# Big runs of 16256 columns in place of 16384 in a streaming binary cross entropy

## The chip, the cores and the metric

One core of a Trainium2 chip. The time is that of the device in microseconds, median of several executions. Verdicts are by ratio at 2%. A ratio is the mean time of one kernel's runs over that of the other's runs of the same rounds, so it is not quite the ratio of the medians that are quoted.

Words used below: SBUF is the core's memory on the chip. In the views DVE is VectorE, ACT is ScalarE, POOL is GpSimd and SP is SyncE. All transfers are issued by POOL or SP, each on a queue of its own, and the core's 16 transfer (DMA) engines work for both queues. The page is the summary of one profiled execution; it cuts the span into 40 equal slices and gives busy shares in tenths. A table by stretches gives for each stretch: its bounds and length in us, the busy us (and instructions) of VectorE, ScalarE and POOL, the clock, the share of the transfer engines, GB/s. In short stretches a share can read a little above 1.

## The reference

```python
def setup_inputs():
    return {"pred": uniform(0.01, 0.99, (8192, 8192)) as float32,
            "target": randint(0, 2, (8192, 8192)) as float32}

def reference(pred, target):
    eps = 1e-7
    pred = np.clip(pred, eps, 1 - eps)
    return -(target * np.log(pred) + (1 - target) * np.log(1 - pred))
```

Two inputs and one output of 268.4 MB each. As the target is 0 or 1, the kernel computes -ln |pred + target - 1|.

## The kernel before

The flat tensors are cut into chunks of 128 x w elements; partition p takes w consecutive elements, so a row in memory is w x 4 bytes and the rows of one chunk lie w x 4 bytes apart. Two rings in SBUF hold 32768 columns of predictions (f32, overwritten in place by the result) and of targets (cast to bf16 by the load). A chunk is loaded once the part of the ring that it takes has been stored.

The code is cut (# ...) and condensed; declarations are left out.

```python
RING = 32768
BIG = 16384

def plan(total):
    head = [(8192, [4096, 4096]), (8192, [8192])]
    tail = [(8192, [4096, 4096]), (8192, [4096, 2048, 2048])]
    n = (total - sum(w for w, _ in head + tail)) // BIG
    chunks = head + [(BIG, [BIG // 2] * 2)] * n + tail
    # ...
    return chunks, len(chunks) - len(tail)
# ... in the kernel:
    def dram(flat, k):
        part = flat[cols[k] * P : (cols[k] + widths[k]) * P]
        return part.rearrange("(p w) -> p w", p=P)
    # ...
    def load(k):
        queue = nc.sync if k == 0 else nc.gpsimd
        nc.gpsimd.dma_start(out=span(ring_t, cols[k], widths[k]), in_=dram(target_f, k))
        queue.dma_start(out=span(ring_p, cols[k], widths[k]), in_=dram(pred_f, k))

    def store(k, off, w):
        queue = nc.sync if k >= tail else nc.gpsimd
        # ...
    def front(col, w):      # clip, (t - 1) + p on VectorE; Abs, Ln on ScalarE
    def back(col, w):       # times -1 on VectorE
    # ...
    def load_what_fits():
        while loaded < len(chunks) and cols[loaded] + widths[loaded] <= stored + RING:
            load(loaded); loaded += 1

    def finish_one():
        k, off, w = waiting.pop(0)
        back(cols[k] + off, w)
        if k >= tail:
            store(k, off, w)
        elif off + w == widths[k]:
            store(k, 0, widths[k])
        else:
            return
        stored = cols[k] + off + w
        load_what_fits()
    # ...
        for k, (_, pieces) in enumerate(chunks):
            off = 0
            for w in pieces:
                front(cols[k] + off, w)
                waiting.append((k, off, w))
                off += w
                if len(waiting) > 1:
                    finish_one()
            while waiting and k < tail:
                finish_one()
        while waiting:
            finish_one()
```

The schedule is manual: each engine runs its instructions in the order of this text. In the tail one piece always waits, so `back` and the store of a piece come after the `front` of the next.

## Time and profile before

| | before |
|---|---|
| time, median | 1866.69 us at first, 1867.16 with one more run |
| span of the profiled execution | 1864.5 us |
| transfer engines' share, page's slices | 90% or more in all 40 |
| VectorE, ScalarE busy | 60%, 48% |
| one big run in the steady part | 57.96 to 58.00 us, 434 GB/s |

The prediction shows the lines for these. One view belongs beside them: the timeline of the kernel before, at the issue of the last loads and at the front of the last chunk. Columns: start, duration in us, engine, line, operation, shapes; the bracket is the engine's idle time and what ended it.

```profile
1786.34 0.54 POOL L76 DMA_DIRECT2D ring_p<-in_pred_dram  x1 [30.48 <-DMA out_dram<-ring_p]
...
1787.38 0.55 POOL L76 DMA_DIRECT2D ring_p<-in_pred_dram  x1
...
1828.66 2.29 DVE L86 TENSOR_SCALAR ring_p<-ring_p 128x4096 f32<-128x4096 f32 x1
```

The last two prediction loads go out within about one us of each other, 77 us before the end. The front of the last chunk has no bracket: VectorE did not wait for its data, which had landed 37.4 us after the issue, at 1824.8, about 4 us before.

### The profile page before, as it was taken

Reading aid. Unit: us, or ns where it says so; the run is one execution under the profiler, and the core shown is the slowest. Engines: PE = TensorE matmul, PEld = TensorE weight load, DVE = VectorE, ACT = ScalarE, POOL = GpSimd, SP = SyncE. Lnnn points to the kernel's source line nnn. Section 1 sums busy time; section 2 is a strip of 40 time slices with the busy share of each in tenths; the row PEclk is TensorE's granted clock in tenths of the full one; section 3 lists DMA queues with packets and bytes.
Section 4 is the critical chain, followed back from the end, with each engine's and each line's share of the span. In section 5 each row is a group of like instructions: output and inputs, shape, how many; then the busy total and the mean of one; then the engine's idle time right before and its main releaser. Section 6 shows DMA issues by size and latency. Waiting matters only on the chain.

```text
span 1864.5 us, 601 instructions
## 1 busy us (share of the span) xinstructions
DVE 1121.4 (60%) x205; ACT 899.3 (48%) x138; POOL 58.4 (3%) x103
## 2 busy tenths in 40 slices
DVE  4557654576545765557655576655766556665576
ACT  3366433664346643366433664335653356533566
POOL 1000000000000000000000000000000000000000
DMA  9999999999999999999999999999999999999999
GB/s 303 358 352 337 351 399 370 340 349 344 396 372 349 340 345 401 378 339 350 344 390 378 356 339 340 396 388 340 342 352 380 389 356 339 340 385 393 347 337 394
DMA packets 15124, 671.13 MB, mean 360 GB/s; under 512 B 1680, under 2 KB 1680, under 8 KB 1680
## 3 DMA queue, kind: packets, MB, share of 16 engines
q0 software_dynamic: 14256, 658.51, 98.5%
q1 hardware_dynamic: 864, 12.58, 1.6%
q14 instruction: 4, 0.03, 0.0%
HBM read 536.87 MB, written 268.44 MB: 432 GB/s over the span
## 4 chain that ended last, share of the span: by engine, by line
DMA 33%; issue 25%; ACT 24%; DVE 15%; POOL 1%; POOLq 0%; DVEq 0%; PEldq 0%
DMA ring_p<-in_pred_dram 31%; ACT ring_p L93 12%; ACT ring_p L92 12%; DVE ring_p L89 8%; DVE ring_p L86 4%; DVE ring_p L97 4%; DMA out_dram<-ring_p 1%; DMA ring_t<-in_target_dram 1%; POOL out_dram L80 1%; POOL ring_t L75 0%; POOLq L80 0%; DVEq L89 0%; PEldq L166 0%; POOLq L76 0%; POOLq L75 0%
## 5 line engine op out<-in xcount | busy, mean ns | idle before, releaser
L92 ACT ACTIVATE ring_p<-ring_p 128x8192 f32<-128x8192 f32 (+2 forms) x68 | 450.2, 6621 | 950.1 <-DVE ring_p L89 950.1
L89 DVE SCALAR_TENSOR_TENSOR ring_p<-ring_t,ring_p 128x8192 f32<-128x8192 bf16 (+2 forms) x68 | 556.9, 8190 | 2.5 <-DMA ring_t<-in_target_dram 0.2
L86 DVE TENSOR_SCALAR ring_p<-ring_p 128x8192 f32<-128x8192 f32 (+2 forms) x68 | 283.7, 4172 | 384.7 <-DMA ring_p<-in_pred_dram 384.7
L97 DVE TENSOR_SCALAR ring_p<-ring_p 128x8192 f32<-128x8192 f32 (+2 forms) x68 | 283.9, 4176 | 344.3 <-ACT ring_p L93 344.3
L93 ACT ACTIVATE ring_p<-ring_p 128x8192 f32<-128x8192 f32 (+2 forms) x68 | 450.7, 6628 | 2.2
L80 POOL DMA_DIRECT2D out_dram<-ring_p x32 | 22.3, 696 | 842.7 <-DVE ring_p L97 842.7
L76 POOL DMA_DIRECT2D ring_p<-in_pred_dram x33 | 17.7, 535 | 912.6 <-DMA out_dram<-ring_p 912.6
L75 POOL DMA_DIRECT2D ring_t<-in_target_dram x34 | 18.7, 551 | 0.8 <-PEq L166 0.8
L127 ACT ACT_TABLE_LOAD x1 | 1.3, 1283 | 0.7 <-PEq L155 0.7
L126 DVE MEMSET warm<- 1x8 f32 x1 | 0.1, 65 | 0.8 <-PEq L155 0.8
L127 ACT ACTIVATE warm<-warm 1x8 f32<-1x8 f32 x1 | 0.2, 208 | 0.0
L155 POOL MEMSET const-float32-0.0<- 128x1 f32 x1 | 0.1, 98 | 0.2 <-issue 0.2
L155 POOL MEMSET const-bfloat16-1.0<- 128x1 bf16 x1 | 0.1, 101 | 0.0
L155 POOL MEMSET const-uint8-127<- 128x1 uint8 x1 | 0.1, 99 | 0.0
L155 POOL MEMSET const-float32-1.0<- 128x1 f32 x1 | 0.1, 98 | 0.0
## 6 DMA issues: line engine op xcount, KB each, us to landing
ring_t<-in_target_dram POOLq DMA_DIRECT2D x30, 4096.0 KB, 50.0
ring_p<-in_pred_dram POOLq DMA_DIRECT2D x3, 4096.0 KB, 37.4
ring_t<-in_target_dram POOLq DMA_DIRECT2D x4, 2048.0 KB, 29.4
out_dram<-ring_p POOLq DMA_DIRECT2D x2, 4096.0 KB, 35.9
out_dram<-ring_p SPq DMA_DIRECT2D x3, 2048.0 KB, 16.2
ring_p<-in_pred_dram SPq DMA_DIRECT2D x1, 4096.0 KB, 19.7
out_dram<-ring_p SPq DMA_DIRECT2D x2, 1024.0 KB, 10.7
ring_p<-in_pred_dram POOLq DMA_DIRECT2D x30, 38.4
```

The source lines that it names most:

```text
L75: nc.gpsimd.dma_start(out=span(ring_t, cols[k], widths[k]), in_=dram(target_f, k))
L76: queue.dma_start(out=span(ring_p, cols[k], widths[k]), in_=dram(pred_f, k))
L80: queue.dma_start(out=dram(out_f, k)[:, off : off + w], in_=span(ring_p, cols[k] + off, w))
L86: nc.vector.tensor_scalar(out=p, in0=p, scalar1=EPS, scalar2=1 - EPS, op0=Alu.max, op1=Alu.min)
L89: nc.vector.scalar_tensor_tensor(out=p, in0=t, scalar=1.0, in1=p, op0=Alu.subtract, op1=Alu.add)
L92: nc.scalar.activation(out=p, in_=p, func=Act.Abs)
L93: nc.scalar.activation(out=p, in_=p, func=Act.Ln)
L97: nc.vector.tensor_scalar(out=p, in0=p, scalar1=-1.0, scalar2=None, op0=Alu.mult)
L126: nc.vector.memset(warm, 1.0)
L127: nc.scalar.activation(out=warm, in_=warm, func=Act.Ln)
L155: nc = _bacc.Bacc("TRN2", target_bir_lowering=False, num_devices=1)
```

## The change

The intent: a row pitch of 65536 bytes is a power of two, and the change tries whether the transfers run faster at a pitch that is none. The row pitch is the distance in memory from one row of a chunk to the next. With runs of 127 units of 128 columns the pitch is 65024 bytes. As 128 units no longer divide everything, the head is 63 + 64 units, and the tail 63 + 64 + 32, its last chunk 4096 columns.

```diff
-RING = 32768
-BIG = 16384
+UNIT = 128
+BIG = 127 * UNIT
+RING = 2 * BIG
@@ def plan(total):
-    head = [(8192, [4096, 4096]), (8192, [8192])]
-    tail = [(8192, [4096, 4096]), (8192, [4096, 2048, 2048])]
-    n = (total - sum(w for w, _ in head + tail)) // BIG
-    chunks = head + [(BIG, [BIG // 2] * 2)] * n + tail
-    assert sum(w for w, _ in chunks) == total
-    return chunks, len(chunks) - len(tail)
+    units = [(63, [32, 31]), (64, [64])]
+    tail = [(63, [63]), (64, [64]), (32, [16, 16])]
+    units += [(127, [64, 63])] * ((total // UNIT - 286) // 127) + tail
+    assert sum(w for w, _ in units) * UNIT == total
+    return [(w * UNIT, [x * UNIT for x in pieces]) for w, pieces in units], len(units) - len(tail)
```

## The prediction

> **What bounds the kernel now.** I read four views in this order: the page's slices, the chain of waits in order of time, the table by stretches, and the timeline of the last 110 us. The first question of an elementwise kernel is whether the transfers ever rest.
>
> ```profile
> span 1864.5 us, 601 instructions
> ...
> DVE 1121.4 (60%) x205; ACT 899.3 (48%) x138; POOL 58.4 (3%) x103
> ...
> DMA  9999999999999999999999999999999999999999
> ...
> q0 software_dynamic: 14256, 658.51, 98.5%
> q1 hardware_dynamic: 864, 12.58, 1.6%
> ...
> HBM read 536.87 MB, written 268.44 MB: 432 GB/s over the span
> ```
>
> No compute engine is over 60%, while the 16 transfer engines are at 90% or more in all 40 slices, and the two queues' packets fill 98.5% + 1.6% of the span. The GB/s line of the page counts a target load by the bf16 bytes it writes, so it wobbles and looks low; the last line counts what leaves and enters memory: 805.3 MB. So the bound is transfer time, and the question is only whether the transfers run at their best rate and where they rest.
>
> For the rate I take the time from one issue of a prediction load to that of the same line later, out of the chain in order of time:
>
> ```profile
> 452.33 38.36 DMA ring_p<-in_pred_dram
> ...
> 1612.47 38.38 DMA ring_p<-in_pred_dram
> ...
> 1728.39 38.33 DMA ring_p<-in_pred_dram
> ```
>
> The chain shows every second big run. From 452.33 to 1728.39 are 22 big runs in 1276.06 us, 58.00 us each; the last two take 115.92 us, 57.96 each. Such a run moves 3 x 128 x 16384 x 4 bytes = 25.17 MB, so the steady rate is 434 GB/s of memory traffic. Before 452 us the same view gives 58.55 us (218.15 to 452.33, four runs). A table by stretches says that the transfers do not rest in the steady part and do at the end:
>
> ```profile
> 452.33:1728.39 1276.06, 770.05 (x133) 616.24 (x89) 35.33 (x67) 1.00 1.00 362
> 1806.00:1864.50 58.50, 40.32 (x16) 31.13 (x11) 2.03 (x1) 1.00 0.93 378
> ```
>
> The last two columns are the transfer share and GB/s. At 434 GB/s the whole 805.3 MB take 1855 us. The span is 1864.5, so all start-up, early unevenness and draining together are some 10 us, 0.5%. **No change of shape can gain more than that** unless it raises the 434.
>
> **What the Trainium skill says.** "DMA: Bandwidth & Descriptors", section "Where 436 GB/s comes from", gives 16 ports x 256 bits x 850 MHz = 435.2 GB/s as the ceiling of the path into SBUF. The trace agrees: 434 in the steady part is 99.8% of it. The same page's "Latency and other measured facts" has the row that this change is after: memory row pitches at large powers of two slow copies, 512 KiB to 207 GB/s per direction and 4 MiB to 103, and padding of 4 KiB restores 214. It measures no pitch as short as the 64 KiB here, and the slow case does not fit: 207 + 207 is already 414, and we see 434. The page says too that all queues share the same 16 engines ("Issuing engines are not separate DMA queues"), and that each engine takes turns between queues by packets ("Queues, rings and completion order"). The page before fits the first (98.5% and 1.6% add up to a full span); the second I use below for the end and no view here shows it directly.
>
> **The change part by part.**
>
> (1) *The pitch.* A run's row goes from 65536 to 65024 bytes, in memory and in the ring. There are still 30 big runs, 127 x 128 columns each. Bytes are the same. From the steady part, 24 rows per engine and run in 57.96 us are 2.415 us per row; at the same rate a row of 65024 takes 2.396. If pitch conflicts cost anything now, it can be only the early unevenness: (58.55 - 57.96) x about 7 early runs, some 4 us. The rate in the steady part cannot rise. I credit 1 us of gain.
>
> (2) *More instructions.* The tail has three chunks in place of two, so one more target load and one more prediction load, and one store less on the SP queue (four in place of five). The compute per column is the same. At 0.55 us of issue on a POOL queue that idles by hundreds of us this is nothing.
>
> (3) *The tail.* This is what I expect to show. Before, the last two chunks of 8192 columns together fit just where one big run lay, so both are loaded when the second last big run has been stored, and all loads are queued early. Now the first two tail chunks (63 + 64 units of 128 columns) fill that place, and the last 4096 columns must wait until the **last** big run is stored and its store has landed (their ring place is that run's). Also the vector engine's program order is: front of tail 1, finish of tail 0, front of the last chunk's first half, and only then the finishing multiply of tail 1. So the store of tail 1 (8192 columns) waits for the landing of the last load. The timeline of before gives the durations:
>
> ```profile
> 1766.74 4.43 DVE L86 TENSOR_SCALAR ring_p<-ring_p 128x8192 f32<-128x8192 f32 x1 [12.25 <-DMA ring_p<-in_pred_dram]
> 1771.20 8.69 DVE L89 SCALAR_TENSOR_TENSOR ring_p<-ring_t,ring_p 128x8192 f32<-128x8192 bf16 x1
> ...
> 1793.93 7.01 ACT L92 ACTIVATE ring_p<-ring_p 128x8192 f32<-128x8192 f32 x1
> ...
> 1812.76 2.03 POOL L80 DMA_DIRECT2D out_dram<-ring_p  x1 [24.82 <-DVE ring_p L97]
> ```
>
> Let X be the landing of the last big prediction load, 1766.7 before. From X to the issue of that run's store are 46.0 us. Transfers, at 57.96/3 = 19.3 us per 16384 columns of one stream: before, from X, the store of the run before (19.3), both tail loads of both streams (38.6), the last big store (19.3), the tail stores (19.3): X + 96.5 = 1863.2, and the span ends at 1864.5. So before, the end has no gap at all (the 0.93 is the engines not ending together).
>
> After, X is earlier, as 31 x 2 loads and 29 stores of 1 unit less have been moved by then: 91 x 0.151 = 13.7 us, so X = 1753. Then
> - transfers: store 19.2 and tail loads 38.3, to X + 57.5; last big store (issued X + 45.7), to X + 76.7; its landing lets the last prediction load go, whose target load is queued ahead of it.
> - engines: front of tail 0 from X + 45.7, 12.9 us; ScalarE 13.9; multiply 4.4: its store is issued at X + 77. Tail 1: vector front until X + 72, ScalarE until X + 86.4.
> - the two last loads (9.7 together) and the store of tail 0 (9.5) share the engines by packets: all done at X + 96, the load at about X + 94, at the earliest X + 87 if the store is served after it.
> - front of a 2048 piece 1.2 + 2.3, multiply of tail 1 4.4: its store is issued at X + 102 and moves at about X + 103.5 (start-up latency, an estimate).
> - so the transfers **rest from X + 96 to X + 103.5, 7.5 us**, then 9.7 + 4.8 us for the last stores: X + 118. With 1.3 us to the end of the span: 1872.3.
> The times of before are 2.2 us above its span (1866.7 against 1864.5): 1874.5. Minus the 1 us of (1), plus about 1.5 for engines that do not reach the end together, which a late load makes worse: **1875 us**, 0.4% slower.
>
> **The rivals.**
> - *The pitch does matter*: then the 434 would rise or at least the early 58.55 fall to 57.96. For: the skill's row on pitches, and the early unevenness. Against: 434 is at the ceiling. Full success here with no loss at the tail: 1862.
> - *The tail's load is hidden*: if the last load is served ahead of tail 0's store, it lands at X + 87 and tail 1's store is issued at X + 95, when the transfers are still busy to X + 96. Then the gap is 1 us and the time about 1868. For: it was queued earlier, partly. Against: packets take turns, and the store enters while the target load is still moving.
> - *The odd row hurts*: 65024 bytes might be cut into more or less even packets. Twice the packets at an unchanged rate cost little; but if it cost 1% of the rate, 1855 x 0.01 = 19 us, giving 1894. Against: the tail before, with its shorter rows, ends just where 19.3 us per 16384 columns puts it (X + 96.5), and 65024 is a multiple of 512.
> - *The smaller last chunk helps* by shortening the last drain: the end before has no gap, so there is nothing to shorten.
>
> **Range and chances.** Floor of everything going well 1862, hidden tail 1868, the sum above 1875, a late load with more sharing 1880. The range is 1866 to 1882. Faster by over 2% means below 1829, under the floor of 1855 at the measured ceiling: 0.01. Slower by 2% is above 1904, which needs a worse rate throughout: 0.03. Same: 0.96.
>
> **What would show it.** In the changed profile: time per big run 57.5 us (57.96 x 127/128) in the steady part, i.e. still 434 GB/s; packets of one row each, so about as many as before plus some 300 for the added pair of loads; a stretch near the end with a transfer share well below the 0.93 of before (some 8 us of rest in the last 25); in the timeline a wait of the vector engine for the last prediction load of some 20 us, and the finishing multiply of 8192 columns after it. If the steady time per run is under 57.3 or over 57.8, step (1) is wrong; if the vector engine finds the last load landed, or no rest shows before the last three stores, step (3) is. The prediction as a whole fails if the rate changes.

## The result, and the profile after

The changed kernel took **1875.17 us** (1874.76 to 1875.36, 4 runs) beside 1867.16 for before (4 runs): ratio 1.0042, 95% interval 1.0025 to 1.006. Clear of noise it is 8 us slower.

The page of the changed kernel, the lines that answer to those of before:

```profile
span 1873.6 us, 600 instructions
...
DMA  9999999999999999999999999999999999999997
...
DMA packets 15268, 671.13 MB, mean 358 GB/s; under 512 B 1696, under 2 KB 1696, under 8 KB 1696
...
q0 software_dynamic: 14544, 656.55, 97.8%
q1 hardware_dynamic: 720, 14.55, 1.9%
HBM read 536.87 MB, written 268.44 MB: 430 GB/s over the span
```

The last slice: a 7 where before had a 9. The two shares add up to 99.7% in place of 100.1%. In the chain in order of time, 22 big runs apart:

```profile
448.68 38.27 DMA ring_p<-in_pred_dram
...
1714.51 38.04 DMA ring_p<-in_pred_dram
```

1265.83 us for 22 runs is 57.54 us each, and 3 x 128 x 16256 x 4 bytes in that time is 434 GB/s: the steady rate has not moved. The table by stretches puts numbers on the end (last two columns: share of the transfer engines, GB/s); the second fence is the same 12 us of the kernel before.

```profile
448.68:1714.51 1265.83, 764.16 (x133) 611.54 (x89) 35.33 (x66) 1.00 1.00 362
1806.00:1873.60 67.60, 35.91 (x11) 35.44 (x8) 0.53 (x1) 1.00 0.80 322
1845.00:1857.00 12.00, 8.33 (x4) 3.82 (x2) 0.00 (x0) 1.00 0.06 25
```

```profile
1845.00:1857.00 12.00, 5.82 (x5) 5.27 (x3) 0.00 (x0) 1.00 0.99 421
```

From 1845 to 1857 us the transfers do 6% of what they can: 11.3 us of rest per engine, where before they worked at 99%. The timeline says why:

```profile
1798.31 4.10 POOL L82 DMA_DIRECT2D out_dram<-ring_p  x1 [24.70 <-DVE ring_p L99]
...
1829.61 0.53 POOL L78 DMA_DIRECT2D ring_p<-in_pred_dram  x1 [26.68 <-DMA out_dram<-ring_p]
1831.74 7.03 ACT L95 ACTIVATE ring_p<-ring_p 128x8192 f32<-128x8192 f32 x1
1848.64 1.23 DVE L88 TENSOR_SCALAR ring_p<-ring_p 128x2048 f32<-128x2048 f32 x1 [19.46 <-DMA ring_p<-in_pred_dram]
1849.90 2.29 DVE L91 SCALAR_TENSOR_TENSOR ring_p<-ring_t,ring_p 128x2048 f32<-128x2048 bf16 x1
1852.11 4.42 DVE L99 TENSOR_SCALAR ring_p<-ring_p 128x8192 f32<-128x8192 f32 x1
```

Read it from the top. The store of the last big run is issued at 1798.3. The last prediction load takes that run's place in the ring, so it is issued only at 1829.6, when that store has landed. VectorE waits 19.46 us for it. ScalarE had finished the chunk of 8192 columns at 1831.74 + 7.03 = 1838.8, but its multiply stands in VectorE's order behind the front of the last chunk: it runs at 1852.1, and its store follows at 1856.5. In between the transfer engines have nothing to move.

The whole loss lies here. The last big load landed at 1752.57 in place of 1766.74, 14.2 us earlier, where the bytes moved less by then account for 13.7; and from 1690 to 1844 us the transfer share is 1.00 in both kernels.

### The profile page after: what moved, and what is told of

Read it like the earlier page. It is cut to its first block, busy times and chain, and to the rows that moved or that the text cites. A ratio compares the mean times of both kernels' runs of the same rounds, so it can differ in the third digit from the quotient of the medians. Undisturbed runs are those within 1.5% of the kernel's fastest.

```text
span 1873.6 us, 600 instructions
## 1 busy us (share of the span) xinstructions
DVE 1121.1 (60%) x202; ACT 899.0 (48%) x136; POOL 61.6 (3%) x105
## 4 chain that ended last, share of the span: by engine, by line
DMA 34%; issue 26%; ACT 23%; DVE 15%; POOL 1%; POOLq 0%; DVEq 0%; PEldq 0%
DMA ring_p<-in_pred_dram 32%; ACT ring_p L95 12%; ACT ring_p L94 12%; DVE ring_p L91 7%; DVE ring_p L99 4%; DVE ring_p L88 4%; DMA out_dram<-ring_p 1%; DMA ring_t<-in_target_dram 1%; POOL out_dram L82 1%; POOL ring_t L77 0%; POOLq L82 0%; POOLq L168 0%; DVEq L88 0%; DVEq L91 0%; PEldq L168 0%
## 5 line engine op out<-in xcount | busy, mean ns | idle before, releaser
L94 ACT ACTIVATE ring_p<-ring_p 128x8064 f32<-128x8064 f32 (+3 forms) x67 | 450.1, 6717 | 962.0 <-DVE ring_p L91 962.0
L91 DVE SCALAR_TENSOR_TENSOR ring_p<-ring_t,ring_p 128x8064 f32<-128x8064 bf16 (+3 forms) x67 | 556.8, 8310 | 2.5 <-DMA ring_t<-in_target_dram 0.2
L88 DVE TENSOR_SCALAR ring_p<-ring_p 128x8064 f32<-128x8064 f32 (+3 forms) x67 | 283.6, 4232 | 398.3 <-DMA ring_p<-in_pred_dram 398.3
L99 DVE TENSOR_SCALAR ring_p<-ring_p 128x8064 f32<-128x8064 f32 (+3 forms) x67 | 283.8, 4235 | 342.5 <-ACT ring_p L95 342.5
L95 ACT ACTIVATE ring_p<-ring_p 128x8064 f32<-128x8064 f32 (+3 forms) x67 | 450.5, 6724 | 2.1
L78 POOL DMA_DIRECT2D ring_p<-in_pred_dram x34 | 18.2, 535 | 928.6 <-DMA out_dram<-ring_p 928.6
```

The costliest lines, as they stand in the source:

```text
L88: nc.vector.tensor_scalar(out=p, in0=p, scalar1=EPS, scalar2=1 - EPS, op0=Alu.max, op1=Alu.min)
L91: nc.vector.scalar_tensor_tensor(out=p, in0=t, scalar=1.0, in1=p, op0=Alu.subtract, op1=Alu.add)
L94: nc.scalar.activation(out=p, in_=p, func=Act.Abs)
L95: nc.scalar.activation(out=p, in_=p, func=Act.Ln)
L99: nc.vector.tensor_scalar(out=p, in0=p, scalar1=-1.0, scalar2=None, op0=Alu.mult)
```

## The experiments

Ten kernels ran, in three batches, each compared with the kernel before on the same chip. The first two batches ran on one chip; the third batch ran on another chip. My theory: the pitch does nothing at 64 KiB; the 8 us are the rest at the end, which comes from the late load, what shares the engines with it, and the order on VectorE. The rivals: the odd pitch gained something that the tail took back (or lost something); or the new shape costs time in some other way than by the late load.

| run | median us | ratio to before, 95% |
|---|---|---|
| before, batches 1, 2, 3 | 1866.43, 1866.01, 1867.00 | 1 |
| control (the changed kernel) | 1875.14 | 1.0050 (1.0038 to 1.0063) |
| pitch_even | 1874.62 | 1.0046 (1.0032 to 1.0060) |
| pitch_odd | 1865.61 | 0.9998 (0.9986 to 1.0011) |
| order | 1870.32 | 1.0022 (1.0009 to 1.0035) |
| store_behind | 1867.98 | 1.0012 (0.9998 to 1.0026) |
| split_last | 1869.51 | 1.0017 (1.0005 to 1.0030) |
| pitch_2m | 2005.21 | 1.0747 (1.0727 to 1.0767) |
| pitch_1m9 | 1875.58 | 1.0051 (1.0037 to 1.0064) |
| pitch_512k | 1882.34 | 1.0095 (1.0066 to 1.0124) |
| pitch_128k | 1866.76 | 0.9998 (0.9981 to 1.0015) |

### The yardstick

> The changed kernel once more, as the yardstick of this batch. Both theories: 1875 us, within 1 us of the first measurement, and 1.004 of the kernel before.

1875.14 us: the first measurement holds.

### The pitch alone, both ways

The changed kernel with its big runs 16384 columns apart in memory again. The skipped unit of each row makes the result wrong; bytes moved, instructions and tail stay.

```diff
     def dram(flat, k):
-        part = flat[cols[k] * P : (cols[k] + widths[k]) * P]
-        return part.rearrange("(p w) -> p w", p=P)
+        first, pitch = place(k)   # place: left out here; big runs 128 units apart,
                                  # all other chunks keep their own width as pitch
+        part = flat[first * P : (first + pitch) * P]
+        return part.rearrange("(p w) -> p w", p=P)[:, : widths[k]]
```

> The changed kernel with its big runs, still 127 x 128 columns, laid at a row pitch of 16384 columns (64 KiB) in memory again; one unit of each row is skipped and a few written twice, so the result is wrong on purpose. Bytes, instructions and tail are those of the changed kernel. Theory (the pitch does nothing, all of the loss is in the tail): 1875 us, within 1 us of the control. Rival (the odd pitch gained some us that the tail took back): slower than the control, 1878 to 1880 us, with a longer period in the early big runs.

And the kernel before with its big runs 16512 columns apart, by the same edit:

> The kernel before with its big runs at a row pitch of 16512 columns (66048 bytes) in memory; again some columns are skipped and some written twice, a wrong result on purpose. Bytes, instructions and tail are those of before. Theory (pitch does nothing): 1867 us, within 1 us of before. Rival (64 KiB pitch costs the early unevenness): 1863 to 1864 us.

With the tail of the change, 64 KiB pitch gives 1874.62 beside 1875.14 at 65024 bytes. With the tail of before, 66048 bytes give 1865.61 beside 1866.43 at 64 KiB. Both pairs lie within 1 us, and the ranges of their runs overlap. The chain of the pitch_even run has the same steady period:

```profile
448.20 38.14 DMA ring_p<-in_pred_dram
...
1714.29 38.03 DMA ring_p<-in_pred_dram
```

1266.09 us for 22 runs, 57.55 each, beside 57.54 in the changed kernel. So **the pitch, the reason for the change, is worth nothing that these runs can see (under 1 us)**, and the loss stays when the pitch is put back. The pitch does not explain the slightly longer early runs of before (58.55 us) either, as most of the excess stays without it: at 66048 bytes they were 58.33 (218.01 to 451.31 us, four runs), and among the runs of 16256 columns 57.60 at 64 KiB pitch (217.81 to 448.20) and 57.68 at 65024 (217.98 to 448.68). What they are due to stays open.

### The order on VectorE

```diff
             for w in pieces:
+                while waiting and k == len(chunks) - 1 and off == 0:
+                    finish_one()
                 front(cols[k] + off, w)
```

> The changed kernel with one exchange in the tail: the finishing multiply and store of the 8192-column chunk come before the front of the last chunk, so that store no longer waits for the last load. Theory (most of the loss is the wait of that store behind the last load): the store moves near 1845 us, where the transfers used to stop, and only the last chunk's own chain of some 12 us from the landing of its load at 1848.6 is left beside it; 1868 us (1866 to 1870). Rival (the late load itself sets the end whatever the order): 1873 to 1875 us.

1870.32 us, 4.8 less than the control, though a little over my range. The timeline and the table by stretches of this run:

```profile
1838.71 4.43 DVE L99 TENSOR_SCALAR ring_p<-ring_p 128x8192 f32<-128x8192 f32 x1 [9.62 <-ACT ring_p L95]
1851.03 1.23 DVE L88 TENSOR_SCALAR ring_p<-ring_p 128x2048 f32<-128x2048 f32 x1 [7.90 <-DMA ring_p<-in_pred_dram]
```

```profile
1845.00:1857.00 12.00, 5.90 (x4) 2.35 (x2) 0.00 (x0) 1.00 0.86 370
1857.00:1868.30 11.30, 3.50 (x3) 5.18 (x3) 0.00 (x0) 1.00 0.45 186
```

The multiply now runs at 1838.7, when ScalarE is done, and the 12 us that were empty are 86% filled. But the store that was freed runs beside the last load, which lands at 1851.0 in place of 1848.6, and the last chunk's own chain then keeps the end: the last 11.3 us are 45% filled. So the exchange alone gives back 4.8 of the 8.7 us to the kernel before, and the late load is what keeps the rest of this run.

### What the last load shares the engines with

```diff
-        queue = nc.sync if k >= tail else nc.gpsimd
+        queue = nc.sync if k > tail else nc.gpsimd
```

The store of the first tail chunk moves to the queue in which the last load stands, and stands behind it; VectorE's order is that of the change.

> The changed kernel with the store of the first tail chunk moved from the SP queue to the POOL queue, where it stands behind the last load. Theory (the last load lands late because it shares the engines by packets with that store): the load lands near 1840 us in place of 1848.6, the vector engine's wait for it falls from 19.5 to some 11 us, the 8192-column store is issued near 1849 in place of 1856.5, when the moved store has just been done; the rest of the transfers shrinks from 11 us to 1 or 2 and the time is 1867 us (1866 to 1869). Rival (the load is late because its own place comes free late, and sharing does not matter): it lands at 1847 or later and the time stays at 1873 to 1876 us.

1867.98 us, as the theory had it. The timeline of this run:

```profile
1829.19 0.53 POOL L78 DMA_DIRECT2D ring_p<-in_pred_dram  x1 [26.70 <-DMA out_dram<-ring_p]
1829.71 0.54 POOL L82 DMA_DIRECT2D out_dram<-ring_p  x1
...
1840.33 1.23 DVE L88 TENSOR_SCALAR ring_p<-ring_p 128x2048 f32<-128x2048 f32 x1 [11.59 <-DMA ring_p<-in_pred_dram]
...
1843.80 4.42 DVE L99 TENSOR_SCALAR ring_p<-ring_p 128x8192 f32<-128x8192 f32 x1
```

The load is issued at almost the same moment as in the changed kernel, 1829.2 (1829.6 there), and lands 8.3 us earlier, at 1840.3. Nothing of the load itself changed: only what was queued beside it now stands behind it. In two queues the load and the store landed together, at 1848.6 and 1847.4 (18.2 us after its issue at 1829.2); in one queue they landed one after the other, at 1840.3 and 1849.8 (20.1 us after 1829.7). From 1845 to 1857 us the transfer share of this run is 0.87, or 1.6 us of rest, as expected.

### The load earlier

```diff
-    units += [(127, [64, 63])] * ((total // UNIT - 286) // 127) + tail
+    units += [(127, [64, 63])] * ((total // UNIT - 286) // 127 - 1)
+    units += [(64, [64]), (63, [63])] + tail
```

> The changed kernel with its last big run cut into two chunks of 8192 and 8064 columns, each loaded and stored by itself; the place of the last chunk in the ring comes free when the first of them is stored, and its load starts one half run earlier. Program order on the vector engine and the queue of every store are unchanged. Theory (the loss is the late load, which waits for a store of a whole big run): the last load lands near 1832 us, before the vector engine asks for it, no wait for it is left, and the time is 1868 us (1866 to 1870). Rival (the loss is something else of the new shape, three chunks or rows of 508 x 128 bytes): 1873 to 1876 us.

1869.51 us: within the range, 1.5 over the point. One sentence of the expectation is wrong: VectorE's order did change. As each half is now a chunk of its own, its finishing multiply comes before the front of the next half (multiply of the first half at 1768.80, front of the second at 1773.14), where in the changed kernel both fronts come first (1765.64, then the multiply at 1779.88). There is also one more pair of loads and one more store. All of this is added work or added waiting, so it is not likely to be what gives the gain. The timeline at the front of the last chunk, and the table by stretches:

```profile
1823.04 0.53 POOL L79 DMA_DIRECT2D ring_p<-in_pred_dram  x1 [43.31 <-DMA out_dram<-ring_p]
...
1835.47 1.22 DVE L89 TENSOR_SCALAR ring_p<-ring_p 128x2048 f32<-128x2048 f32 x1
```

```profile
1845.00:1857.00 12.00, 9.01 (x5) 7.68 (x5) 0.00 (x0) 1.00 1.01 434
```

The load lands at 1834.4 (11.4 us after its issue; I had said 1832), only 1 us before the front asks for it. The wait is gone (no bracket at the front), and the empty 12 us are full. The rows are still 65024 bytes, there are still three tail chunks, so the shape itself is cleared of most of the loss. What keeps this run some 3 us over the kernel before was not taken apart; VectorE's changed order may be part of it.

### Where a power of two does cost

```diff
     def dram(flat, k):
-        part = flat[cols[k] * P : (cols[k] + widths[k]) * P]
-        return part.rearrange("(p w) -> p w", p=P)
+        rows = flat.rearrange("(p w) -> p w", p=P)
+        return rows[:, cols[k] : cols[k] + widths[k]]
```

This is the kernel before with a row pitch of 2 MiB, still correct, with the same 64 KiB rows. The figures of the Trainium skill in this and in a later expectation are those of the row that the prediction cites ("DMA: Bandwidth & Descriptors", section "Latency and other measured facts"); 328 and 414 GB/s and the times from them are estimates from it.

> The kernel before with every chunk taken as columns of 128 long rows, so that the row pitch is 2 MiB, a large power of two, for all loads and stores; the result stays right. If what the Trainium skill tells of 2 MiB pitches (164 GB/s per direction) held for rows of 64 KiB that are in flight together with the other streams, 805 MB at 328 GB/s would take some 2450 us. If rows this long hide it, as the steady 434 GB/s at 64 KiB pitch lets one think, 1867 us, within 0.5%.

Neither figure: 2005.21 us, 7.5% slower. Over nearly the same stretch as in the prediction the view of this run, and its chain at two loads 26 big runs apart, are

```profile
452.00:1728.00 1276.00, 712.88 (x122) 560.18 (x80) 33.17 (x62) 1.00 1.00 338
```

```profile
241.45 39.98 DMA ring_p<-in_pred_dram
...
1860.21 40.49 DMA ring_p<-in_pred_dram
```

338 GB/s in place of 362, with the transfer engines busy all the time: they do not wait, the same bytes take longer. Per big run it is 62.26 us, 404 GB/s of memory traffic.

The partner has a pitch as long that is no power of two; it is the changed kernel with

```diff
+        if 2 <= k < tail:
+            block = flat[cols[2] * P : cols[tail] * P].rearrange("(p w) -> p w", p=P)
+            return block[:, cols[k] - cols[2] : cols[k] - cols[2] + widths[k]]
```

> The changed kernel with its 30 big runs as columns of one block whose rows are 3810 x 128 columns long, a pitch of 1.86 MiB that is no power of two; the result stays right. It is the partner of the 2 MiB run. Theory (no pitch effect away from large powers of two): 1875 us, within 0.3% of the changed kernel. If long pitches as such cost time, power of two or not: as slow as the 2 MiB run.

1875.58 us, the time of the changed kernel, and 57.58 us per big run (448.48 to 1715.16 us, 22 runs). So the length of the pitch alone does not cost. What sets the slow run apart is the power of two; its rows are 65536 in place of 65024 bytes too, which at 64 KiB made no difference but was not tried at these pitches. Two more pitches, in the kernel before (g is 8, or 2):

```diff
+        i = (k - 2) // g * g + 2
+        if k >= 2 and i + g <= tail:
+            block = flat[cols[i] * P : cols[i + g] * P].rearrange("(p w) -> p w", p=P)
+            return block[:, cols[k] - cols[i] : cols[k] - cols[i] + widths[k]]
```

> The kernel before with 24 of its 30 big runs taken in three blocks of eight, so that their row pitch is 512 KiB; the rest keeps 64 KiB and the result stays right. It asks from which pitch the loss of the 2 MiB run (62.3 us per big run in place of 58.0) sets in. If a pitch of 512 KiB costs as much as 2 MiB: 24 x 4.3 = 103 us, 1969 us. If, as with the 207 GB/s that the Trainium skill tells of this pitch, the loss is slight beside our ceiling (2 x 207 = 414 against 434, 5%): 24 x 2.9 = 70 us at most, 1936 us. If long rows hide it at this pitch: 1866 us.

> The kernel before with its 30 big runs taken in 15 blocks of two, a row pitch of 128 KiB, twice that of before; the result stays right. If the loss starts just above 64 KiB, slower than 1875 us; if it belongs to much larger pitches, 1866 us, within 0.2% of before.

At 512 KiB the time is 1882.34 us, 15 us over before, less than any figure I had written for a loss; one of its four runs took 1893. At 128 KiB it is 1866.76, as before. The chain of the 512 KiB run shows that its loss fades: 60.07 us per run from 223.68 to 463.96 us, but 57.96 from 934.43 to 1398.10, though those runs have the same pitch. At 2 MiB it does not fade. Why it fades at one and not at the other stays open.

## Why the prediction was right

1875 us was said and 1875.17 measured. The mechanism was right and the size near (the span was said to grow by 7.8 us and grew by 9.1); that the times agree to 0.2 us is luck. By its steps:

- **The bound.** Right. The steady rate stayed at 434 GB/s: 57.54 us per run beside 57.5 said, so the odd row, a rival, costs nothing. One reading does not hold, though: the 434 was set beside a ceiling of the ports into SBUF, but it counts bytes at the memory. On the SBUF side, where targets are written as bf16, the same stretch moved 362 GB/s. So "99.8% of the ceiling" is not like with like. What the runs show is that no pitch tried took the steady part above 434.
- **The pitch.** No cost of a pitch of 64 KiB shows, as said. The 1 us of credit was wrong: the two pitch experiments show none.
- **More instructions.** Right that they cost nothing. The check on packets was off: I said some 300 more, there are 144, as I counted the two loads (288) and not the store that goes (144).
- **The tail.** Right in kind, and shown by three runs that each go for one cause (the third with the side effects named above): the order gives back 4.8 us, the sharing 7.2, the early load 5.6 (differences of medians to the control). These do not add up, as each shortens the same rest. In size: X was 1752.6 (said 1753); the load landed at X + 96.0 (said X + 94), as it shared the engines with the store to the end; the multiply's store was issued at X + 104 (said X + 102). VectorE waited 19.5 us (said some 20). The rest per engine was 11.3 us (said 7.5), because most engines stop some us before the slowest one, by which X and all landings are counted (the share is 0.44 from 1844 to 1848 us and 0.00 from 1848 to 1856); between the last landing and the next store lie only the 8 us from 1848.6 to 1856.5.
- **The corrections.** The sum gave a span of 1872.3 us, and 1873.6 was measured: 1.3 more. From span to time 2.2 us were added, where it is 1.6 (the 2.2 set a median beside the span of another execution, whose own time of 1866.26 is 1.8 above it): 0.6 less. The 1 us of credit for the pitch is not there: 1 more. The 1.5 us for engines that end apart are not seen, as the share is still 1.00 from 1871 to 1872 us and 0.01 in the next us: 1.5 less. These four errors add up to 0.2 us.
- **The rivals.** "The last load is served ahead" was put at about 1868: the run that forces it gave 1867.98. "The smaller last chunk helps" did not show: the last slice is emptier. No run tests it alone.

## What to carry to other kernels

Before padding a pitch, test whether it costs anything: a power-of-two pitch need not. With rows of 64 KiB it was harmless at 64 and 128 KiB, cost 0.95% at 512 KiB on three quarters of the data, and 7.5% at 2 MiB. If only the pitch is in question, change only the pitch: here it was the new tail that cost. When sizes in a ring are changed, look at what no longer fits: a remainder chunk that takes the place of the last big run is loaded only after that run's store has landed, and in a fixed instruction order everything behind its front waits with it. A late critical load may do better ahead of a store in its own queue than beside it in another: here that was worth 7.2 us.

## What the Trainium skill lacked or had wrong

- "DMA: Bandwidth & Descriptors", section "Latency and other measured facts", the row on power-of-two pitches: it starts at 512 KiB, for tiles of 16 KiB rows. These runs add rows of 64 KiB with two loads and a store in flight: no loss at 64 KiB (0.9998 between 66048 and 65536 bytes) and at 128 KiB (0.9998), 0.95% for three quarters of the data at 512 KiB, 7.5% at 2 MiB. Its 164 GB/s per direction at 2 MiB would be 328 in all, an estimate from the row; here it was 404. So the loss is not set by the pitch alone. The row length, the mix of streams and the issuing queues differ from the page's; which of them matters was not tested. A pitch of 1.86 MiB, no power of two, cost nothing; one padded by 4 KiB was not run.
- The same page, section "Queues, rings and completion order": engines take turns between queues by packets. The runs fit this (they do not show the packets one by one), and add what it costs: a load beside a store of the other queue landed 19 us after its issue (1829.6 to 1848.6), and 11 us (1829.2 to 1840.3) with the store behind it.
- "HBM Reference", section "Specifications (TRN2)", gives about 425 GB/s for a core that streams alone; here the steady part kept 434 over 22 runs, loads and stores together, counted at the memory (362 on the SBUF side).
- "DMA: Bandwidth & Descriptors", section "Why a DMA increments its semaphore by 16 and not by 1", says that the engines of one transfer finish independently, but not how far apart: here the mean engine rested 11.3 of the 12 us from 1845 to 1857, where only 8 us lie between the last landing, which counts the slowest engine, and the next store's issue.
